# Attention scores: the second float32r product contracts over 128 rows instead of 64

## The chip, the core and the metric

The kernel runs on one core of one Trainium2 chip. The metric is the device time of one execution in microseconds, as the median of several runs. The profiled execution is described by its span, the time from its first to its last instruction. Engines are named as the profile names them: PE is TensorE's matrix products and PEld its weight loads, DVE is VectorE, ACT is ScalarE, POOL is GpSimd, and SP is SyncE, which issues almost all DMAs.

## What is computed

Two layers of a decoder trunk with 512 tokens and 1024 features. Each layer is a half-step SwiGLU feed-forward block, a mixing of tokens by 16 attention heads of 64 features, and a second feed-forward block. The change is in the mixing. Its heads come in three groups: A (softmax, heads 0 to 3), B (softmax over the 128 best keys that an indexer ranks, heads 4 to 7) and C (stick-breaking, heads 8 to 15). Cut to the products that the change touches:

```python
def reference(x, c, w_ada, ...):
    for layer in range(DEPTH):
        ...
        proj = h @ w_in[layer]
        (qa, ka, va, qb, kb, vb, qi, ki, wi, qc, kc, vc) = jnp.split(proj, split_points, axis=-1)
        ...
        oa = moba_attention(qa, ka, heads(va, N_HEADS_A))
        ob = dsa_attention(qb, kb, heads(vb, N_HEADS_B), qi, ki, wi)
        oc = stick_breaking_attention(heads(qc, N_HEADS_C), heads(kc, N_HEADS_C), heads(vc, N_HEADS_C))
        o = jnp.concatenate([oa, ob, oc], axis=2)
        o = (_rms(o).reshape(B, S, D_MIX) * out_g[layer]).astype(x.dtype)
        x = x + g2 * (o @ w_out[layer])

# the scores of each group
logits = jnp.einsum('bqjd,bsd->bqjs', qib, kix)                 # indexer, 8 heads, one key
s = jnp.einsum('bqhd,bqkhd->bhqk', qb, ksel) * scale            # softmax
z = jnp.einsum('bqhd,bshd->bhqs', qb, k) * scale                # stick-breaking
```

## The kernel before

Activations lie feature by token on the chip, in chunks of 128 features by 512 tokens. A float32 operand of a product is carried as two float32r parts, H (the value rounded) and L (what the rounding left), and a large product is H.H + H.L + L.H, three matrix products that add up in PSUM (`mm3`, lines 308 to 310). Weights come in pieces of 512 KB: SP loads `raw` (line 268, three buffers), ACT rounds it to `whi` (line 270), and DVE subtracts to get `wlo` (line 280).

The mixing (`mix`) issues its steps in an order that is written out by hand, the table `PLAN`. A scheduler then puts the instructions into one fixed order for each engine, from that order and from when it reckons buffers and operands to be ready. On the chip each engine takes its own list in order and waits where an operand or a buffer isn't ready yet. Tiles of one tag share a fixed number of buffers; a new tile waits until all who used the old one are done.

A head has 64 features, half the rows of the PE array. The kernel uses the other half to pack two of the three part products into one:

- `put_q` (lines 580 to 589) takes the projected queries of a pair of heads from PSUM. `split_feat` writes H into tile `a` on ACT (line 577) and L into tile `l` on DVE (line 578). Three DMAs on SP (`move`, line 603, 64 partitions each) then build one tile per head: the head's H on its own half of the partitions and its L on the other half.
- `put_k` (lines 591 to 600) does the same for the keys. Here three DMAs build one tile per head that has H on both halves. L stays where it was written, head 0 on rows 0 to 63 and head 1 on rows 64 to 127 of one tile.
- `scores` (lines 605 to 613) issues two products for each block of scores: q tile by k tile over 128 rows, which gives H.H + L.H at once, and then q's H by k's L over the head's own 64 rows, which gives H.L.

All tiles of `put_q` and `put_k` have the tag `qk`, with 12 buffers. `put_q`'s `l` is only read by the moves and becomes free after them.

Scores are made in units (`unit`, then `stick` or `soft`). A unit of index 0 covers query tiles 0 and 1 of both heads of a pair: eight products, four of 256 columns and four of 128. A unit 1 or 2 covers query tiles 2 and 3 of one head: in group C eight products, six of 256 columns and two of 128; in groups A and B four products, two of 512 columns and two of 384. The indexer (`index_heads`, its key from `index_k`) makes one unit of eight products of 256 columns for each four heads, and four products of 512 and 384 columns for each head. In both layers together that is 36 units of eight products and 32 of four.

`finish_pair` (lines 668 to 694) normalises a finished pair. It writes squares into a tile with the tag `of`, two buffers (line 673), sums them on PE (line 679), overwrites the tile with the spread reciprocal roots on DVE (line 333 or 338), transposes it on PE (line 690), and multiplies (line 692). Its buffer is free once the transposes have read it.

Of the kernel before, what the change touches and what calls it, by code (L numbers as in the profile page):

```python
"""Two layers of a conditioned hybrid decoder trunk on one core.

Activations are feature-major ([feature, token]) on chip, so that every weight is used in its own
layout as the stationary operand.  A float32 operand of a large product is carried as two float32r
parts, H = float32r(v) and L = float32r(v - H), and a product is H.H + H.L + L.H in float32 PSUM.

With 512 tokens and blocks of 256 there is at most one past block per query, and the block
top-k always selects it: group A attends to every causal key.  Group B's queries t < 128 have at
most 128 causal keys, all of which its top-128 holds; later tiles rank their keys on chip.
"""  # L10
# [9 lines left out]
F32R = mybir.dt.float32r  # L20
# [6 lines left out]
P = 128  # L27
# [20 lines left out]
# Score tiles of a pair of heads come in three units, each two PSUM banks wide: query tiles 0 and 1  # L48
# of both heads (a bank each), then query tiles 2 and 3 of each head.  A block is (head, index, column in PSUM,
# column in SBUF, width).  # L50
#   with keys on partitions: index is the key chunk, and its columns are the unit's queries from
#   that chunk on; with queries on partitions: index is the query tile, and its columns its keys.
# [15 lines left out]
# Small constants: name, shape in a partition, needed by the first norm or later.  # L68
# [12 lines left out]
def head_chunks(l, f):  # L81
    """d_ff chunks that run side by side at the start of an FFN, while its input is still being made."""
    return list(range(4 if (l, f) == (0, 0) else 2))
# [41 lines left out]
# The order in which the steps of the mixing are issued.  A name that comes again is the next step of  # L125
# the same work: u = a unit of a pair's attention (scores and weights, their transposition or sums,
# outputs), n = norm of a pair's heads, c = q and k of a pair of group C, a and b = q and k of groups
# A and B, i = indexer scores, t = top-k of a query tile, v = values, h = split of a pair's output,
# o = output projection of group C.  w loads a weight piece ahead of its use.
# [53 lines left out]
class Net:  # L183
# [24 lines left out]
    def load(self, names, early):  # L208
        """One tile of small constants: a view per name."""
# [15 lines left out]
    def setup(self):  # L225
        """What the first norm needs."""
# [35 lines left out]
    def fetch(self):  # L262
        """Loads a weight piece and takes its H."""
        nc = self.nc
        self.piece += 1
        n = sum(sum(b - a for a, b in blk[3]) for blk in PIECES[self.piece])
        raw = self.t(self.wp, "raw", [P, 1024], bufs=3)
        nc.sync.dma_start(raw[:, :n], self.io["w"][self.piece, :, :n])
        hi = self.t(self.wp, "whi", [P, 1024], F32R, bufs=5)
        nc.scalar.copy(hi[:, :n], raw[:, :n])  # L270
        self.fetched = n, raw, hi
# [22 lines left out]
    def later(self, us, fn):  # L294
        """Has fn emitted once products of about us more microseconds have been."""
        self.delayed.append([us, fn])
# [16 lines left out]
    def rsqrt(self, ss, shape, inv, r=None, wide=None, pin=False):  # L313
        """With r: of ss * r * r * inv, and times r.  wide: where to write each, repeated."""
# [53 lines left out]
    def ada_first(self):  # L368
        """The shift and scale of the first norm, feature chunk by feature chunk."""
# [8 lines left out]
    def ada_all(self, items):  # L378
        """Modulation vectors, a half of one at a time."""
# [22 lines left out]
    def norm_rms(self, cs, pin=False):  # L402
        """1 / rms of the tokens of cs, a token tile per column."""
# [8 lines left out]
    def norm_wide(self, y, cs):  # L412
        """The same over all partitions."""
# [39 lines left out]
    def ffn_head(self, l, f, halves, prepare=lambda k: None):  # L453
        """First products of the FFN, chunk by chunk of its input."""
# [17 lines left out]
    def ffn(self, l, f, filler, head):  # L472
        """Generator: yields (m, tokens) for each finished part of the output."""
# [68 lines left out]
    def proj_tok(self, l, grp, tiles, evac):  # L542
        """Token-major projection, two steps per token tile: evac(t, psum)."""
# [27 lines left out]
    # Scores contract over 64 features: H.H and L.H go together, as a head's q with H on its own half  # L571
    # of the partitions and L on the other, and its k with H on both.
# [7 lines left out]
    def put_q(self, out, ps, scale=1.0, lo=0):  # L580
        """Features of a pair of heads, from token lo on, in two steps: adds a tile per head."""
        a, b, l = (t[:, lo:] for t in self.new_qk(3))
# [8 lines left out]
    def put_k(self, out, ps, scale=1.0):  # L591
        """Adds a tile of H per head, and one of L, in two steps."""
        a, b, l = self.new_qk(3)
        self.split_feat(ps, scale, a, l)
        out.append((a, b, l))
        yield
        self.move(b[HD:], a[HD:])
        self.move(b[:HD], a[HD:])
        self.move(a[HD:], a[:HD])
# [5 lines left out]
    def scores(self, out, q, k, e, qs, ks, keys_out, start, stop):  # L605
        """Products of a head's q and k: of the columns qs and ks, with keys on partitions or queries."""
        own = slice(64 * e, 64 * e + 64)
        parts = [(q[e][:, qs], k[e][:, ks]), (q[e][own, qs], k[2][own, ks])]
# [6 lines left out]
    def do_rope(self, x, heads, tiles, table):  # L615
        """x: [P, len(tiles), heads, HD] view, rotated in place."""
# [12 lines left out]
    def to_feat(self, src, tiles, put):  # L629
        """src(t): token-major [P, 128] -> put(features by tokens), a step and those of put."""  # L630
# [6 lines left out]
    # Values of a pair of heads: token tile, head, H or L, feature.  A head's H and L are stationary  # L637
    # together, and their products with the weights are added when they leave PSUM.
# [3 lines left out]
    def put_v(self, v, t, ps):  # L642
        """ps: [P, 128] of one pair of heads."""
# [4 lines left out]
    def unit_out(self, pair, u, z, att):  # L648
        """Outputs of a unit, in its score tile, in two steps."""
# [18 lines left out]
    def finish_pair(self, l, pair, cs=slice(0, S)):  # L668
        """RMSNorm of both heads of a pair, in five steps."""
# [26 lines left out]
    def stick(self, pair, q, k, u):  # L696
        """Stick-breaking attention of a unit, keys on partitions, in seven steps."""
# [40 lines left out]
    def soft(self, pair, q, k, u, bias):  # L738
        """Softmax attention of a unit, queries on partitions, in seven steps.  The weights stay without
        their sums' division, which the norm of the heads makes up for.  # L740
        bias(t): [P, 128 * (t + 1)] added to the scores of query tile t."""
# [33 lines left out]
    def index_k(self, l):  # L775
# [30 lines left out]
        def put(ps):  # L806
# [3 lines left out]
            self.qk["ki"] = hi, hi, lo  # L810
# [15 lines left out]
    def index_heads(self, heads):  # L826
        """Adds four indexer heads to the scores, in ten steps."""
# [19 lines left out]
    def topk(self, t):  # L847
        """The top-128 keys of a query tile (lowest index first among equals) as an additive bias."""
# [11 lines left out]
    def gained_rope(self, l, gi):  # L860
        """The rotation's tables times a gain, and the gain of the other features on partitions."""
# [9 lines left out]
    def qk_ab(self, l, name, grp, gi):  # L871
        """Normed, rotated q and k of a pair of heads of group A or B, feature-major."""
# [46 lines left out]
    def finish_half(self, l, cs):  # L919
        """The last pair's norm and split for a token half."""  # L920
# [228 lines left out]
```

## Time and profile before

| | |
|---|---|
| Time, three runs | 2207.52, 2210.2, 2212.14 us; median 2210.2 us |
| Span of the profiled execution | 2206.9 us |
| PE busy | 2171.1 us |
| PEld busy | 1833.1 us |
| DVE busy | 1308.5 us |
| ACT busy | 832.6 us |
| Score products (line 612) | 416, the first at 431.4 us and the last at 1794.2 us |
| DMAs of line 603 | 120 |

The time of the profiled execution as a whole isn't listed apart from its span; the median of the runs is 3.3 us above the span. The two mixings take up about 390 to 760 us and 1440 to 1850 us; the rest is feed-forward, where no score product runs.

Three things help in reading the rows. Consecutive products overlap in the records, since each one's duration includes its passage through the array, so the pace is read from one start to the next and not from a duration. A product's form is written as rows by columns of its stationary operand, then its output: `64*128 64x256` contracts over 64 rows and has 256 columns, `128*128 128x256` over 128 rows. Merged rows of a timeline name the form of their first instruction only.

### The profile page before, as it was taken

How to read it: one execution, taken by the hardware profiler on the slowest of the kernel's cores; microseconds unless marked ns; L12 is line 12 of the kernel's file. 1: busy time of each engine (PE TensorE's matmuls, PEld its weight loads, DVE VectorE, ACT ScalarE, POOL GpSimd, SP SyncE). 2: the span in 40 equal slices, each digit the busy share in tenths (PEclk: the TensorE clock that was granted, in tenths of full speed). 3: DMA queues.
4: the chain of work that ended last, by engine and by line, in shares of the span. 5: the costliest groups of instructions: out<-in, count | busy, mean ns of one | idle time of the engine just before them, and what ended most of it. 6: DMA issues, size and time to landing. Idle time of an engine off the chain costs nothing.

```text
span 2206.9 us, 28693 instructions
## 1 busy us (share of the span) xinstructions
PE 2171.1 (98%) x11280; PEld 1833.1 (83%) x11280; DVE 1308.5 (59%) x2607; ACT 832.6 (38%) x1295; POOL 3.5 (0%) x12
## 2 busy tenths in 40 slices
PE   6999999999999999999999999999999999999999
PEld 5888888878988988888898888887788888888888
DVE  8663744679979777375374333364799787333332
ACT  3422222456655432132242222234565644222220
POOL 0000000000000000000000000000000000000000
PEclk9999999999999999999999999998999999999999
DMA  7873842431222378385243333324222222333331
GB/s 292 272 267 97 288 140 82 111 80 50 76 70 80 120 249 283 99 267 191 86 132 115 96 96 97 96 73 115 58 71 65 75 72 87 96 96 96 97 98 63
DMA packets 82310, 275.45 MB, mean 125 GB/s; under 512 B 9984, under 2 KB 12544, under 8 KB 82176
## 3 DMA queue, kind: packets, MB, share of 16 engines
q1 hardware_dynamic: 80736, 271.53, 39.6%
q8 instruction: 88, 1.44, 0.3%
q10 hardware_dynamic: 1440, 2.10, 0.3%
q14 instruction: 46, 0.38, 0.1%
HBM read 256.55 MB, written 2.10 MB: 117 GB/s over the span
## 4 chain that ended last, share of the span: by engine, by line
PE 92%; DVE 5%; DMA 2%; ACT 1%; issue 1%; DVEq 0%; ACTq 0%
PE z L308 23%; PE z L310 23%; PE z L309 23%; PE z L612 6%; PE b L308 4%; PE b L310 4%; PE b L309 4%; PE z L656 2%; PE z L705 1%; DVE wlo L280 1%; DMA raw<-in_w_dram 1%; PE z L769 1%; DMA qk<-qk 1%; DVE att L568 1%; PE b L679 1%; PE b L633 1%
## 5 line engine op out<-in xcount | busy, mean ns | idle before, releaser
L280 DVE TENSOR_TENSOR wlo<-raw,whi 128x1024 fp32r<-128x1024 f32 (+1 forms) x338 | 412.2, 1220 | 542.1 <-ACT whi L270 540.1
L270 ACT CAST whi<-raw 128x1024 fp32r<-128x1024 f32 (+1 forms) x338 | 354.6, 1050 | 876.0 <-PE z L309 789.1
L308 PE MATMUL z<-hh,whi 128*128 128x512 f32 (+1 forms) x1616 | 597.2, 370 | 6.7 <-DVE xs L986 3.9
L309 PE MATMUL z<-hl,whi 128*128 128x512 f32 (+1 forms) x1616 | 597.2, 370 | 0.5
L310 PE MATMUL z<-hh,wlo 128*128 128x512 f32 (+1 forms) x1616 | 596.2, 369 | 1.3 <-DVE wlo L280 1.3
L308 PEld LDWEIGHTS z<-hh,whi 128*128 128x128 f32 x1616 | 306.0, 190 | 58.6 <-DVE xs L986 4.3
L310 PEld LDWEIGHTS z<-hh,wlo 128*128 128x128 f32 x1616 | 306.1, 190 | 52.7 <-DVE wlo L280 1.8
L309 PEld LDWEIGHTS z<-hl,whi 128*128 128x128 f32 x1616 | 306.4, 190 | 52.1 <-DVE hl L430 1.3
L308 PE MATMUL z<-gh,whi 128*128 128x512 f32 (+1 forms) x792 | 293.5, 371 | 0.0
L309 PE MATMUL z<-gl,whi 128*128 128x512 f32 (+1 forms) x792 | 292.8, 370 | 0.0
L310 PE MATMUL z<-gh,wlo 128*128 128x512 f32 (+1 forms) x792 | 289.1, 370 | 0.0
L349 DVE CUSTOM_DVE_ANT_0 adaw<-adaw,silc 128x1024 f32<-128x1024 f32 x144 | 170.9, 1221 | 30.1 <-DMA adaw<-in_w_ada_dram 30.1
L308 PEld LDWEIGHTS z<-gh,whi 128*128 128x128 f32 x792 | 149.0, 188 | 29.6
L310 PEld LDWEIGHTS z<-gh,wlo 128*128 128x128 f32 x792 | 149.1, 188 | 27.6
L309 PEld LDWEIGHTS z<-gl,whi 128*128 128x128 f32 x792 | 149.1, 188 | 26.5
L308 PE MATMUL b<-whi,hh 128*128 128x256 f32 x544 | 158.1, 291 | 0.0
L309 PE MATMUL b<-wlo,hh 128*128 128x256 f32 x544 | 156.1, 287 | 0.0
L310 PE MATMUL b<-whi,hl 128*128 128x256 f32 x544 | 156.0, 287 | 0.0
L612 PE MATMUL z<-qk,qk 64*128 64x256 f32 (+7 forms) x416 | 138.3, 392 | 1.5 <-DMA qk<-qk 1.5
L612 PEld LDWEIGHTS z<-qk,qk 128*128 128x128 f32 (+1 forms) x416 | 78.5, 189 | 56.9 <-issue 26.6
L506 DVE SCALAR_TENSOR_TENSOR xs<-z,mod,xs 128x512 f32<-128x512 f32 (+1 forms) x72 | 49.7, 691 | 124.5 <-PE z L310 124.4
L308 PEld LDWEIGHTS b<-whi,hh 128*128 128x128 f32 x544 | 105.7, 194 | 1.2 <-issue 0.6
(144 smaller groups left out, 2348.3 us busy)
## 6 DMA issues: line engine op xcount, KB each, us to landing
raw<-in_w_dram SPq DMA_DIRECT2D x332, 512.0 KB, 3.6
adaw<-in_w_ada_dram SPq DMA_DIRECT2D x144, 512.0 KB, 4.7
qk<-qk SPq DMA_DIRECT2D x96, 128.0 KB, 2.2
qk<-qk SPq DMA_DIRECT2D x24, 96.0 KB, 3.0
xs<-in_x_dram SPq DMA_DIRECT2D x4, 512.0 KB, 5.7
raw<-in_w_dram SPq DMA_DIRECT2D x4, 492.0 KB, 3.4
silc<-in_c_dram SPq DMA_DIRECT2D x3, 512.0 KB, 5.1
out_dram<-xs ACTq DMA_DIRECT2D x6, 256.0 KB, 2.0
```

The lines of the kernel that those rows point to most:

```text
L270: nc.scalar.copy(hi[:, :n], raw[:, :n])
L280: self.nc.vector.tensor_sub(lo[:, :n], raw[:, :n], hi.bitcast(F32)[:, :n])
L308: mm(out, l[0], r[0], start=start, stop=False, **kw)
L309: mm(out, l[0], r[1], start=False, stop=False, **kw)
L310: mm(out, l[1], r[0], start=False, stop=stop, **kw)
L349: r = self.nc.vector.tensor_tensor_reduce(w, w, self.silc, 1.0, 0.0, op0=ALU.mult, op1=ALU.add, accum_out=m[:, j:j + 1])
L506: nc.vector.scalar_tensor_tensor(self.x[m][:, cs], ps[:, cs], gate[:, m:m + 1], self.x[m][:, cs], op0=ALU.mult, op1=ALU.add)
L568: nc.vector.tensor_sub(unit_sbuf(lo, u), src, unit_sbuf(hi.bitcast(F32), u))
L612: self.nc.tensor.matmul(out, a, b, start=start and i == 0, stop=stop and i == 1, skip_group_check=True)
L633: self.nc.tensor.transpose(ps[:, t * P:(t + 1) * P], src(t), self.ident)
L656: nc.tensor.matmul(outs[e][:, HT - w:], lhs, a[:, o:o + w], start=i + j == 0, stop=c == KEY_UNITS[u][-1][1] and j == 1, skip_group_check=True)
L679: nc.tensor.matmul(ss[:, i, :], sq[:, t * P:(t + 1) * P], self.bones, start=True, stop=True)
```

## The change

`put_k` now makes four tiles: the two with H on both halves as before, and two more with L on both halves, by three more moves. There are eight `put_k` in a layer, so 48 more DMAs on SP. `scores` uses, for the second product, the whole tile of the head's queries (H and L) and the head's new tile of the keys' L, over 128 rows: it now gives H.L + L.L. The number of products and their columns stay, and so does what DVE and ACT do. `put_q`'s passing tile `l` moves from the tag `qk` to the tag `of`, whose two buffers it now shares with `finish_pair`; this makes room for `put_k`'s fourth tile. For the indexer's key, which is already on both halves, the same L tile is named twice.

```diff
     def put_q(self, out, ps, scale=1.0, lo=0):
-        a, b, l = (t[:, lo:] for t in self.new_qk(3))
+        a, b = (t[:, lo:] for t in self.new_qk(2))
+        l = self.t(self.mp, "of", [P, S], F32R, bufs=2)[:, lo:]
         self.split_feat(ps[:, lo:], scale, a, l)
         out.append((a, b))
         yield
...
     def put_k(self, out, ps, scale=1.0):
-        a, b, l = self.new_qk(3)
+        a, b, l, m = self.new_qk(4)
         self.split_feat(ps, scale, a, l)
-        out.append((a, b, l))
+        out.append((a, b, l, m))
         yield
-        self.move(b[HD:], a[HD:])
-        self.move(b[:HD], a[HD:])
-        self.move(a[HD:], a[:HD])
+        for own, other in ((a, b), (l, m)):
+            self.move(other[HD:], own[HD:])
+            self.move(other[:HD], own[HD:])
+            self.move(own[HD:], own[:HD])
         yield
...
     def scores(self, out, q, k, e, qs, ks, keys_out, start, stop):
-        own = slice(64 * e, 64 * e + 64)
-        parts = [(q[e][:, qs], k[e][:, ks]), (q[e][own, qs], k[2][own, ks])]
+        parts = [(q[e][:, qs], k[i + e][:, ks]) for i in (0, 2)]
         for i, (a, b) in enumerate(parts):
             if keys_out:
                 a, b = b, a
...
             hi, lo = self.new_qk(2)
             nc.scalar.copy(hi, ps)
             nc.vector.tensor_sub(lo, ps, hi.bitcast(F32))
-            self.qk["ki"] = hi, hi, lo
+            self.qk["ki"] = hi, hi, lo, lo
```

Lines behind line 580 stand one to three lines lower after the change: the score product is line 614 and the move line 606.

The scheduler's order stays the same nearly everywhere. Three places show what moves.

The first is SP's list in the first layer, at the keys of the first pair of group C. Tile 3391 is that pair's H (head 0's tile in the end), 3392 the other head's, 3393 is L and 3394 the new tile of L; `raw` are weight pieces. Before:

```order
L603 DMA qk_568_3392<-qk_567_3391 64x512 x2
L268 DMA raw_638_3760<-in_w_dram 128x1024
L603 DMA qk_567_3391<-qk_567_3391 64x512
L268 DMA raw_641_3766<-in_w_dram 128x1024
L268 DMA raw_661_3891<-in_w_dram 128x1024
```

After:

```order
L606 DMA qk_568_3392<-qk_567_3391 64x512 x2
L606 DMA qk_570_3394<-qk_569_3393 64x512 x2
L268 DMA raw_640_3768<-in_w_dram 128x1024
L606 DMA qk_567_3391<-qk_567_3391 64x512
L606 DMA qk_569_3393<-qk_569_3393 64x512
L268 DMA raw_643_3774<-in_w_dram 128x1024
L268 DMA raw_663_3899<-in_w_dram 128x1024
```

Two moves of L now stand ahead of the next weight piece and a third behind it.

The second is PE's list in the first layer, at the end of one unit of group C (tile z_765 before, z_769 after), the transposes of two pairs' norms (line 690, which read the two buffers of the tag `of`) and the next unit (z_775 before, z_779 after). Tile 4463 is the keys' L before; 4475 and 4476 are the two L tiles after. Before:

```order
L612 MATMUL z_765_4592<-qk_694_4100,qk_743_4463 128x128
L705 MATMUL z_765_4592<-rmat_513 128x2x128
L690 MATMUL b_772_4613<-rmat_513,of_705_4209 128x128 x4
L690 MATMUL b_774_4622<-rmat_513,of_658_3884 128x128 x4
L612 MATMUL z_775_4629<-qk_693_4099,qk_741_4461 128x256
L612 MATMUL z_775_4629<-qk_693_4099,qk_743_4463 128x256
```

After:

```order
L614 MATMUL z_769_4608<-qk_697_4112,qk_747_4476 128x128
L707 MATMUL z_769_4608<-rmat_513 128x2x128
L692 MATMUL b_776_4629<-rmat_513,of_708_4221 128x128 x4
L614 MATMUL z_779_4645<-qk_696_4111,qk_744_4473 128x256
L614 MATMUL z_779_4645<-qk_696_4111,qk_746_4475 128x256
L614 MATMUL z_779_4645<-qk_696_4111,qk_744_4473 128x256
L614 MATMUL z_779_4645<-qk_696_4111,qk_746_4475 128x256
L614 MATMUL z_779_4645<-qk_696_4111,qk_744_4473 128x256
L614 MATMUL z_779_4645<-qk_696_4111,qk_746_4475 128x256
L614 MATMUL z_779_4645<-qk_696_4111,qk_744_4473 128x128
L614 MATMUL z_779_4645<-qk_696_4111,qk_746_4475 128x128
L692 MATMUL b_778_4638<-rmat_513,of_660_3892 128x128 x4
```

The second pair's transposes went from ahead of the next unit's eight score products to behind them; first and second products still alternate.

The third is DVE's list at the same place: the split of group A's first queries (line 578 before, 579 after; its L is tile 4604 before and takes an `of` buffer, 4620, after) among the rows of the top-k (lines 853 and 854) and of the two pairs' norms (line 692 before, 694 after). Before:

```order
L857 TENSOR_SCALAR sc1_475_2840<-sc1_475_2840 128x256
L578 SCALAR_TENSOR_TENSOR qk_768_4604<-b_762_4568,late_507,qk_766_4602 128x512
L881 TENSOR_REDUCE qss_752_4526<-rl_764_4581 128x4
L854 MATCH_REPLACE sc2_476_2841<-m8_933_5568,sc2_476_2841 128x384
L665 TENSOR_TENSOR osb_763_4573<-osb_763_4573,z_715_4299 64x256
L853 MAX m8_934_5571<-sc2_476_2841 128x8
L692 SCALAR_TENSOR_TENSOR osb_690_4080<-osb_690_4080,late_507,b_772_4613 128x512
```

After:

```order
L859 TENSOR_SCALAR sc1_475_2840<-sc1_475_2840 128x256
L856 MATCH_REPLACE sc2_476_2841<-m8_939_5592,sc2_476_2841 128x384
L883 TENSOR_REDUCE qss_756_4542<-rl_768_4597 128x4
L855 MAX m8_940_5595<-sc2_476_2841 128x8
L855 MAX m8_958_5724<-sc3_477_2842 128x8
L667 TENSOR_TENSOR osb_767_4589<-osb_767_4589,z_718_4311 64x256
L579 SCALAR_TENSOR_TENSOR of_772_4620<-b_766_4584,late_507,qk_770_4618 128x512
L694 SCALAR_TENSOR_TENSOR osb_693_4092<-osb_693_4092,late_507,b_776_4629 128x512
```

The split went behind five instructions, next to the row that uses the transposes.

## Prediction

> **What bounds the kernel now.** I read the page first, for the engine that sets the time, and then the chain of work that ended last, for the lines on it.
>
> ```profile
> span 2206.9 us, 28693 instructions
> PE 2171.1 (98%) x11280; PEld 1833.1 (83%) x11280; DVE 1308.5 (59%) x2607; ACT 832.6 (38%) x1295; POOL 3.5 (0%) x12
> PE 92%; DVE 5%; DMA 2%; ACT 1%; issue 1%; DVEq 0%; ACTq 0%
> PE z L308 23%; PE z L310 23%; PE z L309 23%; PE z L612 6%; PE b L308 4%; PE b L310 4%; PE b L309 4%; PE z L656 2%; PE z L705 1%; DVE wlo L280 1%; DMA raw<-in_w_dram 1%; PE z L769 1%; DMA qk<-qk 1%; DVE att L568 1%; PE b L679 1%; PE b L633 1%
> ```
>
> PE is the bound, and the 416 score products of L612 alone hold 6% of the chain, about 130 us (0.06 x 2206.9). That is 0.32 us for each, though none is wider than 512 columns and most have 128 or 256. So I looked at their pace, in the timeline of PE around one unit of eight (six of 256 columns, two of 128):
>
> ```profile
> 474.06 0.40 PE L310 MATMUL b<-hh,wlo 128*128 128x512 f32 x1
> 474.29 2.35 PE L612 MATMUL z<-qk,qk 128*128 128x256 f32 x8
> 476.57 0.39 PE L705 MATMUL z<-rmat 128*128 128x256 f32 x1
> 476.92 0.28 PE L309 MATMUL b<-wlo,hh 128*128 128x256 f32 x1
> 477.99 0.28 PE L309 MATMUL b<-wlo,hh 128*128 128x256 f32 x1
> ```
>
> The eight take 2.28 us from their first start to the next line's (474.29 to 476.57). The projection's 256-column products behind them go at 0.119 us each (nine steps from 476.92 to 477.99), with a new weight for each. At that pace the unit would need 6 x 0.119 + 2 x 0.06 (half the columns) = 0.83 us, so it loses 1.45 us, 0.18 for each product. The weight loads of the 512- and 384-column products show where:
>
> ```profile
> 425.89 0.19 PEld L309 LDWEIGHTS b<-hl,whi 128*128 128x128 f32 x1
> 427.02 0.19 PEld L308 LDWEIGHTS b<-hh,whi 128*128 128x128 f32 x1
> ...
> 440.24 0.19 PEld L612 LDWEIGHTS z<-qk,qk 128*128 128x128 f32 x1
> 440.68 0.18 PEld L612 LDWEIGHTS z<-qk,qk 64*128 64x128 f32 x1 [0.25 <-issue]
> 441.10 0.19 PEld L612 LDWEIGHTS z<-qk,qk 128*128 128x128 f32 x1 [0.24 <-issue]
> 441.47 0.18 PEld L612 LDWEIGHTS z<-qk,qk 64*128 64x128 f32 x1 [0.18 <-issue]
> 441.84 0.19 PEld L612 LDWEIGHTS z<-qk,qk 128*128 128x128 f32 x1 [0.19 <-issue]
> ```
>
> In the projection (first two rows, five steps apart, 512 columns) a load follows the last by 0.226 us, under the running product. In the scores each load, of either kind, waits for nothing that the profile names and comes 0.42 or 0.37 us after the last: every step from 128 rows to 64 and back costs about 0.2 us. Four products take 1.60 us (440.24 to 441.84); at the projection's pace they need 2 x 0.226 for 512 columns and 2 x 0.170 (0.226 x 384/512) for 384, 0.79 us.
>
> Is it the change of rows, or something in these products, two that add up in one place? Products of 128 rows that do the same, the unit's outputs, with the same eight widths, show it:
>
> ```profile
> 570.05 1.03 PE L656 MATMUL z<-att,v 128*128 128x256 f32 x7
> 571.01 0.89 PE L612 MATMUL z<-qk,qk 64*128 64x256 f32 x3
> ```
>
> A unit's outputs take 0.96 us (570.05 to 571.01), close to 0.83 and far from 2.28. I take the change of rows as the cause. On this the Trainium skill, "TensorEngine Tiling (Array Packing)", section "Key Properties", says that changing the tiling mode drains TensorE. The trace agrees, with the 0.2 us at each step above; by a rule that counted columns alone there would be nothing to gain.
>
> **The change, part by part.** *The 64-row products go.* All loads become 128-row loads, and the stall goes from every score product: 36 units of eight x 1.45 = 52 us and 32 of four x 0.81 = 26 us, together **78 us of PE time**. The second product's own cost stays: the columns set the pace, and no row of the trace makes a product of 64 rows shorter. L612 is on the chain for 130 us, so nearly all its stalls are on the path; but what is late next?
>
> ```profile
> 425.00:470.00 45.00, 44.65 (x196) 32.12 (x194) 22.55 (x38) 19.57 (x26) 0.00 (x0) 0.96 0.39 103
> 470.00:600.00 130.00, 129.58 (x799) 112.03 (x797) 119.08 (x292) 84.95 (x128) 0.00 (x0) 0.99 0.25 67
> 600.00:705.00 105.00, 104.93 (x696) 90.54 (x695) 84.95 (x255) 61.90 (x148) 0.00 (x0) 1.00 0.26 73
> 1515.00:1560.00 45.00, 43.88 (x176) 31.84 (x175) 19.28 (x30) 18.00 (x24) 0.00 (x0) 0.85 0.37 96
> 1560.00:1690.00 130.00, 129.53 (x769) 110.01 (x768) 116.91 (x279) 83.97 (x125) 0.00 (x0) 0.97 0.25 66
> 1690.00:1800.00 110.00, 109.74 (x737) 95.51 (x738) 90.02 (x275) 63.92 (x152) 0.00 (x0) 1.00 0.26 71
> ...
> 470.00:600.00 130.00, 26.55 (x88) 16.08 (x87) 0.99 0.25 67
> 1560.00:1690.00 130.00, 29.23 (x92) 17.54 (x92) 0.97 0.25 66
> ```
>
> The first six rows are stretches of both mixings: length, then busy time of PE, PEld, DVE, ACT and POOL, the granted clock, and DMA. The last two are L612 alone. **DVE is late next.** From 470 to 600 it is busy 119.1 of 130 us. PE would give back 88 x 78/416 = 16.5 us, which would leave 113.5, less than DVE's work; and both engines take their lists in order. So the stretch can't fall under 119.1, and some of DVE's 10.9 idle us are handovers from ACT that stay; I leave it 5. It gains 6 us, and 10.5 of the 16.5 are lost. From 1560 to 1690: 92 products, 17.3 us from PE, DVE 116.9 + 5, a gain of 8, 9.3 lost. At 600 to 705 and 1690 to 1800 (64 products each by the same units, 12 us) PE would need 93 and 98 us against DVE's 85 and 90, 91 to 92% busy, as full as the stretch before is now (119.1 of 130). I take off 3 us in each, between none and the whole 12. At 425 to 470 and 1515 to 1560 DVE has half its time free and nothing is lost.
>
> *The clock.* It is low in the stretches with many scores:
>
> ```profile
> 446.00:448.00 2.00, 2.00 (x7) 0.89 (x7) 0.00 (x0) 1.65 (x2) 0.00 (x0) 0.75 0.26 107
> 448.00:450.00 2.00, 2.00 (x7) 1.71 (x8) 0.56 (x1) 1.16 (x3) 0.00 (x0) 0.50 0.00 0
> ```
>
> The loss is (1 - clock) x length: 1.8, 1.3, 6.8 and 3.9 us in the four stretches below 1.00, 13.8 in all. PE is busy all through these two rows, 7 products in each, so I put the fall down to the stalled products. Not all dips need come from them: between 0 and 13.8, I take half, 7 us gained. The Trainium skill, "TensorE: Matmul & The Clock Gate", section "What's actually happening", gives two clock states, half and full, and the half one after an idle window. The 0.50 agrees; the idle window doesn't show in these rows. By its rule the dips would come from waits, the 7 us would not be gained, and the time would be 7 us longer.
>
> *The 48 more moves.*
>
> ```profile
> L603 SPq DMA_DIRECT2D qk<-qk x120: 461/462/785, 421.3 to 1781.9; - x120
> ...
>   PE z L612: 1.5, 2
> ...
> DMA to landing us min/median/max: 2.0/2.2/5.7
> ...
> SPq L268 <- DVE wlo L280: 1213.5, 266, 19.7
> ```
>
> A move costs SP 0.46 us, 48 cost 22 us. SP has that time: it stood 1213.5 us waiting to reload weights. The keys' L is ready 3 x 0.46 = 1.4 us later than H, and the weight piece queued between the moves is up to 1 us later, but it waits for DVE anyway. Behind a late L stands the second product, and on PE everything behind that. The old moves held PE twice, for 1.5 us in all. So between 0 and 22 us (every move exposed); nearest to the row of 1.5, I take **3 us**.
>
> *The queries' passing L in a norm buffer.* It takes no instruction, but one of the two buffers must be free before DVE's split, and everything on DVE queues behind it. The one place where the order moved for it:
>
> ```profile
> 570.43 0.75 DVE L578 SCALAR_TENSOR_TENSOR qk<-b,late,qk 128x512 fp32r<-128x512 f32 x1
> ...
> 572.05 1.04 PE L690 MATMUL b<-rmat,of 128*128 128x128 f32 x8
> 573.00 1.39 DVE L692 SCALAR_TENSOR_TENSOR osb<-osb,late,b 128x512 f32<-128x512 f32 x2
> ```
>
> Before, the split runs at 570.43, 2.6 us ahead of L692, which needs the transposes that free the buffer. Now it stands next to L692, which waits for those transposes already. Price: 0 to 2.6 us a layer. I take 0, with the five rows that went ahead of it as cover, and the bound in the range.
>
> **The sum**: -78 + 10.5 + 9.3 + 6 - 7 + 3 = -56 us. The profiled span of 2206.9 becomes 2151; the median of the runs shown is 3.3 us above the span, so **2154 us**.
>
> **The rivals.**
>
> *PE gets nearly all of it.* DVE's idle time goes as far as it can: lost are only 16.5 - 10.9 = 5.6 and 17.3 - 13.1 = 4.2, with the whole 13.8 of the clock and no new wait: 78 - 9.8 + 13.8 = 82, so 2128 us. For it: 6% of the chain is L612. Against it: DVE would have to run without a gap for 119 us.
>
> *More is given back.* The two full stretches gain nothing (-33.8), the clock doesn't rise, the two others lose the whole 12 (-24), and the moves cost 10 of their 22: 78 - 33.8 - 24 - 10 = 10 us gained, 2200 us; halfway to my forecast is 2177. For it: in-order lists couple three engines. Against it: all of L612's 130 us are on the chain now.
>
> *The products don't speed up.* The stall would come from what the score products share (their tile, the adding up in one place), and 128 rows would stall as 64 do. Then only the moves count: 2210 to 2215 us. Against it: L656, 0.96 us.
>
> *Slower, by the norm buffers.* Both buffers are held by waiting norms when DVE reaches a split; DVE stops, and what would end the norms stands behind it or needs PE, which soon waits for DVE.
>
> ```profile
> L673 ACT ACTIVATE of<-osb x18: 412/622/633, 503.2 to 1809.2; 128x512 f32<-128x512 f32 x14, 128x256 f32<-128x256 f32 x4
> ```
>
> The first norm takes its buffer at 503.2 and frees it after the transposes at 572.05, 69 us later. A split that met half of that would wait 34 us in each layer: 2154 + 68 = 2222 us. It decides at 56/2 = 28 us a layer; above that the kernel is slower. For it: this split now stands where it needs a norm that ends. Against it: its distance in the trace is 2.6 us, a tenth of 28.
>
> **How the numbers follow.** The forecast, 40 to 70 us gained: 0.62. PE gets nearly all: 0.16. More is given back: 0.14. The products don't speed up: 0.04, and slower by the buffers: 0.04. A measurement of this kernel can tell some 0.2%, 4.4 us, from no change. Faster takes the first three and a little of the rest, 0.93; same 0.03, slower 0.04. The range goes from just under the full gain, 2126, to 2182, just above the half of what is given back; outside are the end of that case and the last two.
>
> **What will show it.** In the changed profile: a unit of eight takes about 0.9 us from start to start and L612's loads wait for nothing; L612's share of the chain falls from 6% to 2 or 3%. If DVE is next, it is over 95% busy in the scores' middle stretch, with PE waiting there for DVE rows (L568, L717). The clock should stay at 1.00 where scores are dense. Waits of PE or PEld for `qk` moves above 10 us in all, or of DVE's L579 for PE above 5 us, would prove my two small terms wrong; units still at 2.3 us would overturn the forecast.

## The result, and the profile after

The changed kernel takes **2150.5 us** (median of 4 runs, 2149.6 to 2151.9) against 2211.2 us for the kernel before (4 runs, 2207.5 to 2212.5): a ratio of 0.9732, with a 95% interval from 0.9719 to 0.9746, or 60.7 us less. The prediction was 2154 us, in a range from 2126 to 2182.

The head of the page after, then the two lines of its chain (shares by engine, then by line). In the changed kernel the scores' line is L614 (L612 before), the moves L606 (L603), the unit's outputs L658 (L656), the splits L578 on ACT and L579 on DVE.

```profile
span 2149.1 us, 28769 instructions
PE 2095.1 (97%) x11280; PEld 1806.7 (84%) x11280; DVE 1305.0 (61%) x2607; ACT 831.1 (39%) x1295; POOL 3.0 (0%) x12
PE 83%; DVE 12%; ACT 2%; DMA 2%; issue 1%; SPq 0%; ACTq 0%; DVEq 0%
PE z L308 23%; PE z L310 23%; PE z L309 23%; PE b L308 3%; PE b L309 3%; PE b L310 3%; DVE att L568 2%; DVE sc L856 2%; DVE m L855 2%; PE z L614 1%; DVE wlo L280 1%; PE z L658 1%; DMA raw<-in_w_dram 1%; DVE osb L667 1%; PE z L707 1%
```

The number of products is the same, 11280, and PE is busy 76 us less. The scores fell from 6% of the chain to 1%, and DVE rose from 5% to 12%: where scores were on the path, DVE now often is. Here is PE's timeline around the unit of eight that the prediction showed:

```profile
463.52 0.39 PE L310 MATMUL b<-hh,wlo 128*128 128x512 f32 x1
463.75 1.05 PE L614 MATMUL z<-qk,qk 128*128 128x256 f32 x8
464.63 0.33 PE L707 MATMUL z<-rmat 128*128 128x256 f32 x1
```

From start to start it takes 0.88 us (463.75 to 464.63), where it took 2.28. The weight loads show why; PEld's timeline after:

```profile
437.70 0.19 PEld L310 LDWEIGHTS b<-whi,hl 128*128 128x128 f32 x1
437.82 1.59 PEld L614 LDWEIGHTS z<-qk,qk 128*128 128x128 f32 x8
```

Eight loads of the scores now stand in one row (1.59 us for eight), without the 0.18 to 0.25 us of "issue" ahead of each that the rows before had.

The windows after, cut at the same instructions of PE's order as the six stretches of the prediction (so 425.5 here is 425 there, 461 is 470, 580.5 is 600, and so on; length, busy PE, PEld, DVE, ACT, POOL, clock, DMA):

```profile
425.50:461.00 35.50, 33.49 (x196) 29.10 (x195) 22.75 (x39) 18.70 (x26) 0.00 (x0) 1.00 0.52 133
461.00:580.50 119.50, 114.20 (x798) 105.12 (x797) 118.14 (x292) 84.75 (x128) 0.00 (x0) 1.00 0.32 86
580.50:678.40 97.90, 95.97 (x696) 89.78 (x695) 84.12 (x254) 60.80 (x146) 0.00 (x0) 0.98 0.34 91
1488.30:1519.70 31.40, 28.92 (x177) 25.55 (x176) 19.33 (x30) 17.27 (x23) 0.00 (x0) 1.00 0.54 139
1519.70:1637.70 118.00, 112.57 (x769) 102.44 (x768) 116.07 (x280) 83.61 (x126) 0.00 (x0) 1.00 0.32 83
1637.70:1741.10 103.40, 101.19 (x739) 94.98 (x738) 89.09 (x275) 63.35 (x150) 0.00 (x0) 0.98 0.34 91
```

Against the lengths before, the six gain 9.5, 10.5, 7.1, 13.6, 12.0 and 6.6 us, together 59.3; the rest of the kernel is 1.5 us longer, which makes the 57.8 us between the spans. In the second and fifth row DVE is busy 118.14 of 119.50 us and 116.07 of 118.00, 99 and 98%: there DVE's own list leaves next to nothing more to gain.

### The profile page after: what moved, and what is told of

It reads as the page before. It is cut to its first block, busy times and chain, and to the rows that moved or that the text cites. A ratio compares the mean times of both kernels' runs of the same rounds, so it can differ in the third digit from the quotient of the medians.

```text
span 2149.1 us, 28769 instructions
## 1 busy us (share of the span) xinstructions
PE 2095.1 (97%) x11280; PEld 1806.7 (84%) x11280; DVE 1305.0 (61%) x2607; ACT 831.1 (39%) x1295; POOL 3.0 (0%) x12
## 4 chain that ended last, share of the span: by engine, by line
PE 83%; DVE 12%; ACT 2%; DMA 2%; issue 1%; SPq 0%; ACTq 0%; DVEq 0%
PE z L308 23%; PE z L310 23%; PE z L309 23%; PE b L308 3%; PE b L309 3%; PE b L310 3%; DVE att L568 2%; DVE sc L856 2%; DVE m L855 2%; PE z L614 1%; DVE wlo L280 1%; PE z L658 1%; DMA raw<-in_w_dram 1%; DVE osb L667 1%; PE z L707 1%
## 5 line engine op out<-in xcount | busy, mean ns | idle before, releaser
L270 ACT CAST whi<-raw 128x1024 fp32r<-128x1024 f32 (+1 forms) x338 | 354.3, 1049 | 871.0 <-PE z L309 788.3
L309 PEld LDWEIGHTS b<-wlo,hh 128*128 128x128 f32 x544 | 104.2, 191 | 0.2
L310 PEld LDWEIGHTS b<-whi,hl 128*128 128x128 f32 x544 | 104.2, 191 | 0.0
```

The lines of the kernel that those rows point to most:

```text
L309: mm(out, l[0], r[1], start=False, stop=False, **kw)
L310: mm(out, l[1], r[0], start=False, stop=stop, **kw)
```

## The experiments

Each run was taken beside runs of the kernel before on the same chip; their median is given with it, and the ratio is to them.

**1. The moves and the buffer stay, the rows go back to 64.**

```diff
-        parts = [(q[e][:, qs], k[i + e][:, ks]) for i in (0, 2)]
+        own = slice(64 * e, 64 * e + 64)
+        parts = [(q[e][:, qs], k[e][:, ks]), (q[e][own, qs], k[2 + e][own, ks])]
```

> The changed kernel with its four key tiles, its 48 more moves and its norm-buffer use, but with the second product over the head's own 64 rows again (the kernel before's arithmetic). My theory, that the whole gain is the stall at each step between 128 and 64 rows: the gain goes, the 416 score products take about 134 us from start to start again (68.6 in the changed kernel), and what remains against the kernel before is the price of the moves and buffers alone, 0 to 10 us: 2211 to 2221 us. Rival, that the gain comes from the tiles and the order that the scheduler makes of them: it stays near 2151 us.

Measured: 2217.9 us (10 runs) against 2210.5, ratio 1.0027 [1.0006, 1.0048]. From start to start the score products take 138.8 us again. The whole gain hangs on the rows; what was added for it costs some 6 to 7 us by itself (1 to 11 by the interval).

**2. The kernel before, with its 64-row products put in a row.** Each unit issues all products of 128 rows, then all of 64. Nothing is moved or copied more, and the second product still contracts over 64 rows.

```diff
-        for e, c, o, _, w in blocks:
-            self.scores(z[:, o:o + w], q, k, e, ..., True, o % 512 == 0, False)
+        for i in range(2):
+            for e, c, o, _, w in blocks:
+                self.scores(z[:, o:o + w], q, k, e, ..., True, o % 512 == 0, False, (i,))
...
```

The two other places that call `scores` have the same loop, and its last argument picks the first or the second product.

> The kernel before, with one thing changed: a unit issues all its 128-row products first and then all its 64-row products, so that the rows change twice in a unit and not at every product. No move, buffer or product is added. My theory, a stall of 0.18 to 0.2 us at each change of rows: about 136 changes (68 units x 2) in place of 416, so PE gets back 78 x 280/416 = 52 us, the score products take some 82 us from start to start (134 before), and with DVE as the next bound in the middle stretches the time is 2165 to 2180 us. Rival, that each product of 64 rows is slow by itself and delays the next: nothing is gained, 2207 to 2213 us, 134 us from start to start.

Measured: 2153.6 us (2151.6 to 2155.0), ratio 0.9735 [0.9711, 0.9758]: as fast as the change to within the intervals, without one of its moves. It is a miss on the fast side: I had expected 2165 to 2180 us. PEld's timeline in this kernel, at two units of four, one of eight, and what follows:

```profile
438.31 0.19 PEld L310 LDWEIGHTS b<-whi,hl 128*128 128x128 f32 x1
438.43 0.31 PEld L612 LDWEIGHTS z<-qk,qk 128*128 128x128 f32 x2
439.04 0.29 PEld L612 LDWEIGHTS z<-qk,qk 64*128 64x128 f32 x2 [0.30 <-issue]
439.64 0.30 PEld L612 LDWEIGHTS z<-qk,qk 128*128 128x128 f32 x2 [0.31 <-issue]
440.25 0.29 PEld L612 LDWEIGHTS z<-qk,qk 64*128 64x128 f32 x2 [0.30 <-issue]
440.85 0.90 PEld L612 LDWEIGHTS z<-qk,qk 128*128 128x128 f32 x8 [0.31 <-issue]
...
441.45 0.30 PEld L612 LDWEIGHTS z<-qk,qk 64*128 64x128 f32 x4
441.83 0.19 PEld L706 LDWEIGHTS z<-rmat 128*128 128x128 f32 x1
```

In the units of four the gap stands ahead of each **change** of rows and nowhere between loads of one kind, be they of 64 rows or of 128. So it isn't the 64 rows that are slow, nor the adding up in one place: it is the switch. From 438.43 to 440.85 there are two units of four (512 and 384 columns) with four switches; they take 2.42 us, 2 x 0.79 at the projection's pace, so 0.21 us a switch, as before ((1.60 - 0.79)/4 = 0.20). There are only half as many.

The row of 440.85 is a unit of eight (four products of 256 columns, four of 128), named by its first load; the last four of its loads have 64 rows, and a narrower window shows them (441.45): four in 0.30 us, where two took 0.29. The two heads' 64-row products, on the two halves of the partitions, go side by side; by the records, 40 of the 64-row products in this kernel start within 7 ns of the one before, and in the kernel before none does. That is two for each unit that holds both heads, so 20 of the 36 units of eight. A unit of index 0 takes 0.88 us here (the median of those at full clock), where it took 2.17; a unit of one head of group C 1.12 for 2.28.

Summed over the records, from each score product's start to the start of the next product, all 416 take 134.2 us in the kernel before, 76.2 here (I had expected 82) and 68.6 in the change. So 58.0 us are saved here, and the spans differ by 57.2 (2206.9 to 2149.7). The change saves 7.6 us more in the products and gains no more time by it. In the two middle stretches, cut at the same instructions, DVE sets the time of both kernels: here it is busy for 118.35 of 120.4 and 115.89 of 118.8 us. And in the two late ones this kernel is shorter than the change, 97.1 and 102.5 us against 97.9 and 103.4; what the shared buffer does there is told below.

**3. DVE made lighter, in the kernel before and in the change.** Of the 16 rounds of a top-k on DVE, 4 are left, so that 32 keys in place of 128 are taken out.

```diff
-            nc.vector.max(m8, sc)
-            nc.vector.match_replace(sc, m8, sc, TAKEN)
+            if i < 4:
+                nc.vector.max(m8, sc)
+                nc.vector.match_replace(sc, m8, sc, TAKEN)
```

> The kernel before without 12 of the 16 rounds of the top-k on DVE for each query tile (only 32 of the 128 keys are taken out), so DVE has some 85 us less to do in the two mixings. Theory, that before the change PE alone sets the pace and DVE nearly does from 470 to 600 us: a small gain, 2195 to 2208 us. It is there to be compared with the same cut in the changed kernel.

> The changed kernel with the same cut of the top-k. Theory, that DVE takes back what PE gains in the middle stretches: with a lighter DVE the change brings more than the 60.7 us that it brought, 72 to 85 us against the other cut kernel, so 2115 to 2130 us, and the DVE rows go from the chain. Rival, that the missing part (78 us by pace, 60.7 measured) was lost to the moves and buffers or was never there: the two cut kernels differ by 58 to 63 us still, 2135 to 2148 us.

Measured: the cut kernel before, 2212.5 us (10 runs), ratio 1.0003 [0.9990, 1.0016]; the cut change, 2143.3 us (4 runs), ratio 0.9685 [0.9657, 0.9713]. The first is a miss: I expected 2 to 15 us from it and there is nothing, so DVE's top-k held nobody up before (DVE was busy 66.2 us less, not 85: 1242.3 for 1308.5). The second is a miss of my theory too: 2143.3 us lies outside its 2115 to 2130 and inside the rival's 2135 to 2148, and the two cut kernels differ by 69.2 us, between the theory's 72 to 85 and the rival's 58 to 63. In the change the cut is worth 7.2 us (2150.5 to 2143.3): DVE takes back that much. Some 8 us of the 17.3 that are missing from the 78 were never there: even between the two cut kernels the score products go only from 134.8 to 64.5 us, 70.3 less. The windows of the cut change, for the two middle stretches:

```profile
460.60:576.40 115.80, 114.10 (x798) 105.17 (x797) 90.71 (x199) 84.40 (x128) 0.00 (x0) 1.00 0.34 88
1517.90:1631.80 113.90, 111.83 (x768) 102.21 (x767) 89.24 (x194) 83.22 (x126) 0.00 (x0) 1.00 0.33 87
```

With DVE busy for 90.7 and 89.2 us only, the stretches still take 115.8 and 113.9 us, 3.7 and 4.1 less than the change: then PE sets the pace, busy 114.1 of 115.8 and 111.8 of 113.9.

**4. The change with a buffer of their own for the queries' passing low parts**, from the twelve of q and k.

```diff
-        a, b = (t[:, lo:] for t in self.new_qk(2))
-        l = self.t(self.mp, "of", [P, S], F32R, bufs=2)[:, lo:]
+        a, b, l = (t[:, lo:] for t in self.new_qk(3))
```

> The changed kernel, but the queries' passing L takes one of the 12 qk buffers as before the change, none of the norm's. Theory one, that the shared norm buffers cost something (DVE waited 6.8 us for the moves that free them, and PE 4.1 us for moves): a few us faster than the changed kernel, 2144 to 2149. Theory two, that the fourth key tile needs the room: with three tiles for the queries and four for the keys in 12 buffers, the splits wait for score products to end, and it is 5 to 30 us slower, 2156 to 2181. No difference: 2149 to 2152.

Measured: 2146.7 us (2145.9 to 2147.9), ratio 0.9705 [0.9682, 0.9728]. No run of it is as slow as the fastest of the change (2149.6), though the two intervals of the ratio just overlap. It is the fastest kernel here that leaves nothing out: sharing the norm's buffer costs some 4 us, and twelve buffers are enough.

**5. The same two parts one at a time, on the kernel before.** Moves alone (products of 64 rows, the queries' low part in its old buffer):

```diff
-        a, b, l = self.new_qk(3)
+        a, b, l, m = self.new_qk(4)
...
-        self.move(b[HD:], a[HD:])
-        self.move(b[:HD], a[HD:])
-        self.move(a[HD:], a[:HD])
+        for own, other in ((a, b), (l, m)):
+            self.move(other[HD:], own[HD:])
+            self.move(other[:HD], own[HD:])
+            self.move(own[HD:], own[:HD])
...
-        parts = [(q[e][:, qs], k[e][:, ks]), (q[e][own, qs], k[2][own, ks])]
+        parts = [(q[e][:, qs], k[e][:, ks]), (q[e][own, qs], k[2 + e][own, ks])]
```

> The 48 more moves alone: the second product contracts over 64 rows of its own again, and the queries' passing low part has its old buffer; only the keys' low parts are made for both heads, by three more moves a split. With the shared norm buffer as well this cost 7 us over the kernel before (2217.9 against 2210.5 us). Theory one, by which the shared buffer has about 4 us of that: the moves alone cost 2 to 4 us, 2212 to 2215 us. Theory two, that all of it is the moves' (the weight pieces behind them in SP's queue come later): 2216 to 2219 us. Theory three, that the moves are free, as SP stands idle over half of the time: within 1 us of the kernel before.

And the buffer alone, with the products and moves of before:

```diff
-        a, b, l = (t[:, lo:] for t in self.new_qk(3))
+        a, b = (t[:, lo:] for t in self.new_qk(2))
+        l = self.t(self.mp, "of", [P, S], F32R, bufs=2)[:, lo:]
```

> The kernel before with nothing but the buffer changed: the queries' passing low part takes one of the two buffers of the norm's squares. No product and no move is changed. Theory one, that the shared buffer makes the norm of a unit wait for a split's moves and so costs PE time by itself: 3 to 5 us slower than before, 2213 to 2216 us. Theory two, that it waits only because the faster products bring the norm closer to the split: within 1 us of the kernel before.

Measured, both against 2210.4 us (23 runs): moves alone 2210.3 us (12 runs), ratio 1.0001 [0.9988, 1.0014]; buffer alone 2215.8 us (12 runs), ratio 1.0029 [1.0016, 1.0043]. The moves are free there, to within some 3 us by the interval, where I had thought 2 to 4 us of them, and most of the first experiment's loss is the buffer's. PE's timeline and then its windows in the kernel with the buffer alone, at the one wait of PE between 600 and 720:

```profile
692.70 0.28 PE L657 MATMUL z<-att,v 128*128 128x256 f32 x1
694.04 1.05 PE L680 MATMUL b<-ones,of 128*128 128x2 f32 x8 [1.06 <-ACT of L674]
...
692.00:696.00 4.00, 2.94 (x22) 2.52 (x20) 3.06 (x5) 1.48 (x3) 0.00 (x0) 1.00 0.63 163
696.00:700.00 4.00, 4.00 (x17) 3.07 (x17) 2.22 (x12) 0.37 (x1) 0.00 (x0) 0.69 0.82 241
700.00:704.00 4.00, 4.00 (x10) 2.37 (x10) 2.71 (x9) 3.25 (x10) 0.00 (x0) 0.50 0.07 27
704.00:708.00 4.00, 4.00 (x16) 3.42 (x16) 1.27 (x6) 0.04 (x1) 0.00 (x0) 0.53 0.00 0
708.00:712.00 4.00, 4.00 (x22) 2.92 (x21) 3.34 (x14) 3.66 (x8) 0.00 (x0) 1.00 0.00 0
```

PE stands 1.06 us for the norm's squares (L674 on ACT, whose output tile is the shared buffer). Then the clock is at 0.69, 0.50 and 0.53 for 12 us: a loss of 1.2 + 2.0 + 1.9 = 5.1 us behind a wait of 1.1. The kernel before has no wait there and a clock of 1.00. But this doesn't show that the wait made the clock fall. The same trace has an equal fall, 1.6 + 2.0 + 1.6 us, where no row of PE's waits stands between 436 and 456:

```profile
444.00:448.00 4.00, 4.00 (x12) 2.67 (x11) 2.33 (x4) 1.06 (x2) 0.00 (x0) 0.61 0.65 206
448.00:452.00 4.00, 4.00 (x10) 2.53 (x10) 0.41 (x1) 2.44 (x4) 0.00 (x0) 0.50 0.00 0
452.00:456.00 4.00, 4.00 (x12) 3.10 (x12) 3.17 (x5) 1.94 (x3) 0.00 (x0) 0.61 0.31 74
```

Over all its runs this kernel has a mean clock of 0.9868, the kernel before 0.9893. Among the runs of the kernel before, 0.001 of the clock goes with 1.9 us. So of the 6.6 us between the two means (2217.1 and 2210.5) some 4.7 go with the lower clock, and some 2 remain at the same clock.

**6. The keys' new moves on another queue**: the kernel of experiment 4, with the three moves of L and its copy issued by POOL.

```diff
         for own, other in ((a, b), (l, m)):
-            self.move(other[HD:], own[HD:])
...
+            eng = self.nc.sync if own is a else self.nc.gpsimd
+            self.move(other[HD:], own[HD:], eng)
...
```

> The change with the queries' low part in a buffer of its own (2146.7 us), and the three added moves of each split of keys issued from POOL's queue, which is nearly empty, in place of SP's, where the weight pieces are issued. The computation is the same. Theory one, that the moves' price lies in SP's queue (1.4 us per split for moves and weight pieces behind them): 2143 to 2146 us. Theory two, that the price is not there: 2146 to 2148 us. Theory three, that POOL issues a move later than SP does, so that the second product waits: above 2149 us.

Measured: 2163.0 us (2159.4 to 2168.6), ratio 0.9786 [0.9768, 0.9805], 16 us slower than with all moves on SP's queue, as theory three had it. From the page, the DMA issues (count, KB, median us from issue to landing), and from the waits of this kernel:

```profile
qk<-qk SPq DMA_DIRECT2D x96, 128.0 KB, 2.2
qk<-qk POOLq DMA_DIRECT2D x48, 128.0 KB, 3.9
...
PE z L614 <- DMA qk<-qk: 20.5, 11, 4.2
```

The same 128 KB land 3.9 us after an issue by POOL and 2.2 us after one by SP, and PE waits 20.5 us for moves, up to 4.2 us at once. The same row of the kernel with all moves on SP, where the line is L613:

```profile
PE z L613 <- DMA qk<-qk: 5.3, 6, 1.5
```

PE waits 15.2 us more for them, nearly all of the 16. So the moves cost little only as long as they come early: 1.7 us later, they hold up the second product.

## Why the prediction was right, step by step

**The stall: right in mechanism and place.** The forecast rested on "every step from 128 rows to 64 and back costs about 0.2 us". Experiment 2 shows the change of rows to be the cause, at 0.20 to 0.21 us a switch, and experiment 1 that nothing else of the edit gains. A unit of eight came out at 0.88 us for the 0.9 forecast, and "the products don't speed up" falls. The row of L656 that I read as a whole unit's outputs names seven products, not eight; they need 0.72 us at the projection's pace (5 x 0.119 + 2 x 0.06), and with the switch behind them the 0.96 still bears the reading out.

The size was too large. The score products gave up 65.6 us from start to start (134.2 to 68.6), not 78. At full clock and without waits, units of index 0 went from 2.17 to 0.88 us, those of one head of group C from 2.28 to 0.90, units of four from about 1.5 to 0.85; over all units that is some 70. PE's waits at the score products, 1.5 us before and 5.7 after, take the rest. I had given all 36 units of eight the 1.45 us of one kind, had read the units of four at 1.60, and had let nothing remain above the projection's pace.

**DVE late next: right, but its gaps were too large.** I left DVE 5 us idle in each middle stretch, for 124.1 and 121.9 us (119.1 + 5 and 116.9 + 5). They took 119.5 and 118.0, with DVE idle for 1.4 and 1.9 us. That is 8.5 us more gain than forecast, with the 78 the largest error in the sum. The idle time that I took for handovers was slack that DVE had because PE was late: once PE had no stall, DVE hardly waited. The waits of DVE in the change, from 461 to 580, are one row in all:

```profile
DVE sc L844 <- ACT tf L841: 0.2, 1, 0.2
```

So of the 16.5 and 17.3 us that I had PE give, 6.0 and 5.3 were not had, for my 10.5 and 9.3. Part of that was never there: from start to start the score products of the two stretches gave up 12.9 and 14.6 us (25.6 to 12.7 and 28.5 to 13.9). By experiment 3 DVE's top-k holds back 3.7 and 4.1.

**The four other stretches: a little less than forecast.** By the steps of the prediction their products give back 78 - 16.5 - 17.3 = 44.2 us, less 6 for DVE and 3 for the moves: 35.2. They gained 9.5 + 7.1 + 13.6 + 6.6 = 36.8, but that holds the clock: before they lost 1.8 + 6.8 us to it, after 2.0 + 2.1 (0.02 of 97.9 and of 103.4), so 4.5 of the 36.8 are the clock's and 32.3 the products' and their waits'. The cause that I gave for the 3 us each in the two late stretches, "DVE as full", is not borne out: with the light DVE the same stretches are no shorter. The kernel of experiment 4 is shorter there, 96.3 and 101.8 us, at a clock of 1.00:

```profile
580.30:676.60 96.30, 94.82 (x696) 88.30 (x695) 84.87 (x257) 60.60 (x146) 0.00 (x0) 1.00 0.34 93
1634.40:1736.20 101.80, 99.97 (x740) 93.45 (x738) 90.61 (x279) 63.12 (x150) 0.00 (x0) 1.00 0.36 95
```

That is 1.6 us in each, 3.2 of the 5.0 us between the two spans. What the four stretches fell short by lies in the 78 itself: from start to start their score products gave up 38.0 us (9.2, 9.9, 9.2 and 9.7), not 44.2.

**The buffer: a term of 0 that is some 4 us, and sought at the wrong place.** I looked at the split next to L692. The waits of the changed kernel (us in total, times, longest):

```profile
DVE of L579 <- DMA qk<-of: 6.8, 2, 3.5
PE b L681 <- ACT of L675: 3.3, 2, 1.7
PE z L614 <- DMA qk<-of: 2.5, 2, 1.3
PE z L614 <- DMA qk<-qk: 1.6, 2, 1.2
```

The first row is DVE waiting for the moves of a split before to give a buffer back; at L692 PE waits 1.4 us in all for the split that moved there. The sign that I had named, L579 waiting over 5 us for PE, did not come: it waits 6.8 us, but for moves. The wait that costs PE is the second, where a norm's squares come late. The squares don't wait for a buffer. ACT's rows in the change, and then at the same pair in the kernel of experiment 4:

```profile
658.43 1.05 ACT L270 CAST whi<-raw 128x1024 fp32r<-128x1024 f32 x1 [3.36 <-DMA raw<-in_w_dram]
659.51 0.37 ACT L666 COPY osb<-z 64x256 f32<-64x256 f32 x1
660.36 0.63 ACT L675 ACTIVATE of<-osb 128x512 f32<-128x512 f32 x1 [0.48 <-DVE osb L667]
...
656.66 0.37 ACT L665 COPY osb<-z 64x256 f32<-64x256 f32 x1 [1.52 <-PE z L657]
658.12 1.06 ACT L270 CAST whi<-raw 128x1024 fp32r<-128x1024 f32 x1 [1.09 <-DMA raw<-in_w_dram]
659.09 0.62 ACT L674 ACTIVATE of<-osb 128x512 f32<-128x512 f32 x1
```

With the shared buffer the copy of the pair's last outputs (L666) stands behind the rounding of a weight piece (L270) in ACT's list, which waits 3.36 us for its piece to land; the squares stand behind both. Without it the copy (L665) comes first. The second layer shows the same in both kernels, with a wait of 3.52 us at L270. So the price comes by the order that goes with the shared buffer; no run changes that order alone.

The clock falls behind the wait. The windows of the change around it, and then behind the wait in the second layer:

```profile
656.00:660.00 4.00, 3.50 (x19) 2.73 (x17) 2.48 (x5) 1.42 (x2) 0.00 (x0) 1.00 0.75 194
660.00:664.00 4.00, 2.96 (x22) 2.96 (x23) 3.91 (x7) 1.00 (x2) 0.00 (x0) 0.89 0.82 206
664.00:668.00 4.00, 4.00 (x22) 3.66 (x21) 2.81 (x7) 1.53 (x2) 0.00 (x0) 0.68 0.80 257
668.00:672.00 4.00, 4.00 (x25) 3.42 (x24) 3.87 (x21) 2.75 (x11) 0.00 (x0) 1.00 0.00 0
...
1724.00:1728.00 4.00, 4.00 (x24) 4.00 (x24) 2.83 (x7) 0.37 (x1) 0.00 (x0) 0.58 0.86 248
```

The loss is 0.4 + 1.3 us, and 1.7 in the second layer. The kernel of experiment 4 waits 0.5 us in all for its squares, and its clock is 1.00 in both stretches (the rows above). Over the runs, though, the clock of the two kernels is the same, 0.997 as the mean of four runs each, and at 0.998 the change took 2149.6 and 2150.1 us, the kernel of experiment 4 2146.4. So the 4 us or so between them are more the waits' than the clock's. In all the buffer's price, some 2 us a layer, lies inside the bound that I gave (0 to 2.6 us a layer); the choice of its lower end was wrong.

**The moves: 3 us was about right**, for a reason that shows only with fast products. In the waits above PE stands 4.1 us for moves, where it stood 1.5 before, but 2.5 of that are for the queries' moves, which are not new. With fast products and no new move (experiment 2) the row is

```profile
PE z L612 <- DMA qk<-qk: 2.4, 3, 1.0
```

and with the new moves, in the kernel of experiment 4, it is 5.3 us. So the new ones cost about 3 us, if nothing else between these two kernels bears on it; on the slow products the same moves cost nothing (experiment 5).

**The clock: in direction right.** The four stretches that lost 13.8 us to it now run at 1.00. Of the 7 us that I took, 4.5 show in the stretches that PE sets, net of the new dips; in the other two DVE sets the time, and the clock can add nothing there. The prediction's other reading, that dips come from waits, fits the two new dips only: the old ones of the four stretches went although PE is idle there more than before (2.0 of 35.5 us for 0.35 of 45 in the first).

**The sum.** The products and moves of the four stretches gave 2.9 us less than forecast (32.3 for 35.2), the clock 2.5 less, the middle stretches 8.5 more (22.5 for 14), and the rest of the kernel took 1.5 more. Together 57.8 for 56: the nearness of the total owes much to terms that cancelled. The score products gave up 65.6 us for the 78; and of what they gave up in the middle stretches (12.9 and 14.6) only 5.0 us were not had, where I had counted 19.8.

**The rivals.** "PE gets nearly all" had the middle right: DVE did run nearly without a gap, and the middle stretches gained 22.5 of the 24 us that DVE stood idle there before (10.9 + 13.1). Its 82 us also wanted 44 us from the other stretches, the whole clock beside, and no new wait, and these gave 36.8 in all. "More is given back" and "slower by the buffers" fell: the longest wait of a split was 3.5 us, a tenth of what the latter needed.

## What to carry to other kernels

Products of 64 rows among products of 128 cost some 0.2 us at each change between them here, so first try to put those of one kind in a row: that had the same gain for nothing. An engine's idle time in a stretch that another engine holds up is mostly slack, not handover: take its busy time as the floor, with 1 to 2% on top. A buffer that two steps share can cost time though nothing waits for the buffer: look at what moved in the order of every engine's list, here a copy on ACT that came to stand behind a weight piece not yet landed.

## What the runs showed that was not expected

The clock fell behind waits far shorter than I had thought: in the change, PE stood 1.54 and 1.71 us for a norm's squares, and each time a fall followed that cost 1.7 us. In the kernel with the shared buffer alone a fall of 5.1 us followed a wait of 1.06 us, but an equal one came with no wait ahead of it, and none followed its other such wait, of 0.81 us in the second layer. So the link of wait and fall is seen in the change and not tested by itself, and what sets the length of a fall stays open. The Trainium skill, "TensorE: Matmul & The Clock Gate", section "HAM oscillation — how this bites in real kernels", warns of idle gaps of TensorE above some 3.4 us; the two waits of the change are about half as long at most, and the clock fell all the same, so here the measurement decides.

Products of 64 rows on different halves of the partitions ran side by side as soon as they stood next to each other (experiment 2). The Trainium skill, "TensorEngine Tiling (Array Packing)", section "Key Properties", says that tiles operate independently and can load and multiply in parallel; the four loads in 0.30 us agree.

A move that POOL issues lands 1.7 us later than the same move from SP (3.9 against 2.2 us), and 48 of them cost 16 us.
